# Row projection with running-maximum record count: 384-row tiles in four slots and one hardware loop per engine, in place of 512-row tiles in three slots

## The chip, the cores and the metric

The kernel runs on one core of one Trainium2 chip. The metric is the device time of one execution in microseconds; lower is better. Most times below are medians of 4 or 5 executions. A ratio is the mean time of one kernel's fast runs over that of the other's fast runs of the same rounds, so it is not quite the ratio of the medians. Engines: PE multiplies matrices, DVE, ACT and POOL work on vectors, SP issues nearly all transfers. A *slot* is a buffer in SBUF that holds one tile. *Queued* means issued and not yet landed.

## The reference

```python
B, S, D = 8, 2048, 4096              # float32
proj = (x @ w).squeeze(-1)           # x: B,S,D   w: D,1
cm = np.maximum.accumulate(proj, axis=1)
is_record = (proj >= cm).astype(np.float32)
return np.cumsum(is_record, axis=1)
```

Each of the 16,384 rows of x (16 KB each, 268.4 MB in all) is read once and multiplied with one vector. The result is 64 KB. There are two float32 operations for every 4 bytes read, so reading x is the first suspect for the limit.

## The kernel before

Positions 0 to 1919 of each batch are handled in four *groups* of 512, 512, 512 and 384 positions. A group has eight tiles, one per batch. Each of the 128 partitions takes r neighbouring rows of a tile, so one transfer has 128 pieces of r x 16 KB. The last 128 positions (the tail) come in tiles of 64 positions of 2 batches.

```python
RS = (4, 4, 4, 3)          # rows per partition in each group
NS = 3                     # slots of R = 4 rows: 3 x 64 KB per partition
VC = 2816                  # DVE takes columns 0..2815, POOL and ACT the rest

def at(g, t):              # the slot of tile t of group g
    return xbuf[(t if g < NL else t + NS - 1) % NS]

def user_before(g, t):     # the tile that must be finished before t may overwrite its slot
    if t >= NS:
        return t - NS, g + 1
    if g == NL:
        return B - NS + t, g
    return max(u for u in range(B) if u % NS == t), g

# SP, in this order; SP blocks at each wait
i = SY.dma_start(out=at(g, t)[:, : r * D], in_=x[...].rearrange("(p r) d -> p (r d)", r=r)
    ).then_inc(xs[t], 16)
u, n = user_before(g, t)
if n: i._wait_ge(*(free(u, n)))

# DVE: one product with a sum for each row; "go" starts POOL on the tile
for t in range(B):
    if r == R:
        V.wait_ge(xs[t], 16).then_inc(go, 1)      # 512-row groups: when the tile has landed
    for j in range(r):
        i = dot(...)
        if j == 0 and r < R:
            i._wait_ge(xs[t], 16).then_inc(go, 1) # last group: when DVE's first product ends
        elif j == 1:
            i.then_inc(xs[t], -16)
    i.then_inc(fr[t], 1)
# POOL multiplies the other columns, ACT sums them, and then the slot is free.
# ... (cut: PE brings a group's sums into rows; DVE does two scans and a compare; the tail)

with V.Fori(0, NL): ...    # a hardware loop for the three 512-row groups on each engine,
group_dots(RS[-1], NL)     # the last group written out behind it
```

A hardware loop uses the same addresses in each pass, so in the first three groups tile t always sits in slot t mod 3. Eight tiles are no multiple of three. At a group boundary, tile 0 therefore waits for tile 6 of the group before, not for tile 5, which is free one tile earlier.

## Time and profile before

The kernel before takes 631.57 us (median of 3 executions, 631.42 to 631.84). The first fence holds lines of its profile's page: the span, the busy tenths of the 16 DMA engines in 40 slices, the packets, the instruction packets, the costliest groups (busy us, mean ns | idle us before, and what ended it), and the transfers (count, KB each where it is one size under 8 MB, median us from issue to landing).

```profile
span 630.0 us, 1182 instructions
...
DMA  9999999999999999999999999999999999999995
...
DMA packets 6579, 268.55 MB, mean 426 GB/s; under 512 B 768, under 2 KB 1040, under 8 KB 1584
...
q14 instruction: 3, 0.02, 0.0%
...
L127 DVE CUSTOM_DVE_ANT_0 xall<-xall,w_v 128x2816 f32<-128x2816 f32 (+3 forms) x133 | 388.4, 2974 | 187.8 <-DMA xall<-in_x_dram 187.8
L287 POOL TENSOR_TENSOR xall<-xall,w_sb 128x1280 f32<-128x1280 f32 x120 | 344.9, 2909 | 250.2 <-POOLq L290 250.2
...
xall<-in_x_dram SPq DMA_DIRECT2D x8, 6144.0 KB, 30.5
...
xall<-in_x_dram SPq DMA_DIRECT2D x24, 45.0
```

Read the DMA row first: full from the first slice to the last but one. DVE's wait line agrees: it waits for data and nothing else in front of its products.

The timeline of DVE shows the rhythm (start us, duration us, engine, line, operation; in brackets the idle time before it and what ended it). First two neighbouring 512-row tiles, then two 384-row tiles of the last group:

```profile
198.15 3.09 DVE L127 CUSTOM_DVE_ANT_0 xall<-xall,w_v 128x2816 f32<-128x2816 f32 x1 [6.52 <-DMA xall<-in_x_dram]
...
217.50 3.09 DVE L127 CUSTOM_DVE_ANT_0 xall<-xall,w_v 128x2816 f32<-128x2816 f32 x1 [7.23 <-DMA xall<-in_x_dram]
...
512.69 3.09 DVE L127 CUSTOM_DVE_ANT_0 xall<-xall,w_v 128x2816 f32<-128x2816 f32 x1 [5.42 <-DMA xall<-in_x_dram]
...
527.24 3.09 DVE L127 CUSTOM_DVE_ANT_0 xall<-xall,w_v 128x2816 f32<-128x2816 f32 x1 [5.43 <-DMA xall<-in_x_dram]
```

8 MiB each 19.35 us and 6 MiB each 14.55 us (14.53 in most pairs) are both 433 GB/s. The Trainium skill, page "DMA: Bandwidth & Descriptors", section "Where 436 GB/s comes from", gives 435.2 GB/s as the ceiling of the 16 SBUF ports. The trace agrees to half a per cent, so I take the stream to be at its ceiling: only time in which it moves fewer bytes can be lost or won.

This is the first group boundary: ACT finishes tile 6, SP then issues tile 0 of the next group, and tile 7 is taken up by DVE.

```profile
151.58 1.27 ACT L133 ACTIVATE xall<-xall 128x1280 f32<-128x1280 f32 x1 [1.50 <-POOL xall L287]
...
152.97 0.33 SPq L171 DMA_DIRECT2D xall<-in_x_dram  x1
...
159.44 3.09 DVE L127 CUSTOM_DVE_ANT_0 xall<-xall,w_v 128x2816 f32<-128x2816 f32 x1 [7.23 <-DMA xall<-in_x_dram]
```

When tile 0 is issued at 152.97, only tile 7 is still in the queue, and it lands within 6.5 us (DVE takes it at 159.44). Inside a group about a tile more, some 26 us in all, is queued at each issue.

### The profile page before, as it was taken

The page shows a single profiled execution, that of the slowest core. Times are in us where ns is not written, and L with a number is a line of the kernel's source. Part 1 is how long each engine was busy: PE and PEld are TensorE (multiplying, and loading weights), DVE is VectorE, ACT ScalarE, POOL GpSimd, SP SyncE. Part 2 cuts the span into 40 slices and gives each one's busy share as a digit, 9 for nine tenths or more (in the row PEclk, how much of TensorE's full clock was granted, in tenths as well). Part 3 has the DMA queues.
Part 4 walks back from the last instruction along what each step waited for, and adds up shares of the span by engine and source line. Part 5 has one row for each costly group of instructions (what it writes and reads, how often), then busy time and mean ns, then how long its engine had stood idle before and what let it go on. Part 6 is the DMA issues. An engine that isn't in the chain of part 4 may idle for free.

```text
span 630.0 us, 1182 instructions
## 1 busy us (share of the span) xinstructions
PE 31.7 (5%) x108; PEld 15.1 (2%) x108; DVE 406.9 (65%) x292; ACT 180.4 (29%) x273; POOL 370.1 (59%) x147
## 2 busy tenths in 40 slices
PE   8000000000010000000010000000002000000031
PEld 3000000000010000000010000000001000000010
DVE  0755676546785557755579555676557966655897
ACT  1222332123322233222233222332223232232353
POOL 0555676446765557755567555576555766666685
PEclk9999999999999999999996555555555555555555
DMA  9999999999999999999999999999999999999995
GB/s 400 399 466 399 466 408 458 421 442 433 433 441 424 445 424 441 425 445 420 449 416 454 412 458 408 458 408 458 408 425 437 444 418 437 444 415 440 416 424 230
DMA packets 6579, 268.55 MB, mean 426 GB/s; under 512 B 768, under 2 KB 1040, under 8 KB 1584
## 3 DMA queue, kind: packets, MB, share of 16 engines
q1 hardware_dynamic: 6560, 268.50, 98.8%
q10 hardware_dynamic: 16, 0.02, 0.0%
q14 instruction: 3, 0.02, 0.0%
HBM read 268.45 MB, written 0.07 MB: 426 GB/s over the span
## 4 chain that ended last, share of the span: by engine, by line
POOL 52%; issue 38%; DMA 6%; PE 2%; DVE 1%; SPq 0%; POOLq 0%; ACT 0%; ACTq 0%
POOL xall L287 52%; DMA xall<-in_x_dram 6%; PE w_v L231 2%; PE ps L231 0%; DVE xall L127 0%; SPq L199 0%; DMA w<-in_w_dram 0%; POOLq L290 0%; ACT w L242 0%; PE ps L373 0%; DVE cm_l L143 0%; DVE cnt_l L149 0%; DVE ps L146 0%; ACT xall L133 0%; DVE masked L365 0%
## 5 line engine op out<-in xcount | busy, mean ns | idle before, releaser
L127 DVE CUSTOM_DVE_ANT_0 xall<-xall,w_v 128x2816 f32<-128x2816 f32 (+3 forms) x133 | 388.4, 2974 | 187.8 <-DMA xall<-in_x_dram 187.8
L287 POOL TENSOR_TENSOR xall<-xall,w_sb 128x1280 f32<-128x1280 f32 x120 | 344.9, 2909 | 250.2 <-POOLq L290 250.2
L133 ACT ACTIVATE xall<-xall 128x1280 f32<-128x1280 f32 (+1 forms) x130 | 162.8, 1252 | 429.7 <-POOL xall L287 417.1
L319 PE MATMUL ps<-identity,small 128*8 128x128 f32 x60 | 13.1, 410 | 572.0 <-PEq L316 572.0
L133 ACT ACTIVATION_READ_ACCUMULATOR xall<-xall 128x1 f32 x130 | 24.2, 186 | 0.0
L343 POOL TENSOR_TENSOR xall<-xall,w_sb 128x1280 f32<-128x1280 f32 (+1 forms) x8 | 21.6, 2704 | 2.8 <-DMA xall<-in_x_dram 2.8
L319 PEld LDWEIGHTS ps<-identity,small 128*8 128x8 f32 x60 | 7.5, 128 | 578.8 <-issue 574.8
L143 DVE TENSOR_TENSOR_SCAN cm<-ps,cm,small 8x512 f32<-8x512 f32 (+1 forms) x5 | 6.1, 1216 | 14.1 <-PE ps L319 14.1
L231 PE MATMUL w_v<-w,identity 8*128 8x512 f32 x14 | 12.1, 1056 | 0.0
L127 DVE DVE_READ_ACCUMULATOR2_ANT small<- 128x1 f32 x133 | 10.8, 82 | 0.0
L253 DVE MEMSET ps<- 8x512 f32 x1 | 0.5, 485 | 15.5 <-ACT w L242 15.5
L149 DVE TENSOR_TENSOR_SCAN cnt<-ps,cnt,small 8x512 f32<-8x512 f32 (+1 forms) x5 | 6.1, 1217 | 0.2
L373 PE MATMUL ps<-fold,masked 128*8 128x64 f32 x32 | 4.6, 303 | 20.1 <-ACT masked L361 13.2
L231 PEld LDWEIGHTS w_v<-w,identity 8*128 8x128 f32 x14 | 4.6, 332 | 7.3 <-issue 7.3
L239 ACT COPY w_sb<-w_v 128x768 f32<-128x768 f32 x1 | 0.8, 799 | 11.4 <-PE w_v L231 11.4
L146 DVE TENSOR_TENSOR ps<-ps,cm 8x512 f32<-8x512 f32 (+1 forms) x5 | 3.3, 660 | 0.2
L373 PEld LDWEIGHTS ps<-fold,masked 128*8 128x8 f32 x32 | 2.5, 112 | 22.4 <-ACT masked L361 14.6
L361 ACT ACTIVATE masked<-fold,small 128x8 f32<-128x8 f32 x9 | 2.5, 297 | 0.2
L231 PE MATMUL ps<-w,identity 8*128 8x512 f32 x2 | 2.1, 1136 | 2.6 <-DMA w<-in_w_dram 2.6
L238 ACT ACT_TABLE_LOAD x1 | 1.3, 1283 | 2.7 <-DVE fold L249 2.7
L245 DVE TENSOR_REDUCE fold<-identity 128x2 f32<-128x128 f32 x1 | 0.3, 286 | 2.1 <-POOL cnt L224 2.1
L343 POOL TENSOR_TENSOR xall<-xall,w 128x352 f32<-128x352 f32 (+1 forms) x2 | 1.5, 766 | 0.2 <-DMA xall<-in_x_dram 0.2
(23 smaller groups left out, 7.0 us busy)
## 6 DMA issues: line engine op xcount, KB each, us to landing
xall<-in_x_dram SPq DMA_DIRECT2D x8, 6144.0 KB, 30.5
xall<-in_x_dram SPq DMA_DIRECT2D x6, 2048.0 KB, 39.5
xall<-in_x_dram SPq DMA_DIRECT2D x1, 1200.0 KB, 33.5
xall<-in_x_dram SPq DMA_DIRECT2D x1, 848.0 KB, 35.1
xall<-in_x_dram SPq DMA_DIRECT2D x1, 752.0 KB, 36.3
xall<-in_x_dram SPq DMA_DIRECT2D x1, 576.0 KB, 37.1
xall<-in_x_dram SPq DMA_DIRECT2D x24, 45.0
xall<-in_x_dram SPq DMA_DIRECT2D x1, 352.0 KB, 17.4
```

What stands on the lines that cost most here:

```text
L127: return V.tensor_tensor_reduce(out=xsl, in0=xsl, in1=wsl, scale=1.0, scalar=0.0, op0=ALU.mult, op1=ALU.add, accum_out=dst,)
L133: return A.activation(out=xsl, in_=xsl, func=ACTF.Copy, accum_out=dst)
L143: V.tensor_tensor_scan(out=cm_, data0=src, data1=low, initial=cm0, op0=ALU.max, op1=ALU.max,)._wait_ge(psr, base).then_inc(psr, 1)
L146: V.tensor_tensor(out=src, in0=src, in1=cm_, op=ALU.is_ge)._wait_ge(psr, base + 1).then_inc(psr, 1)
L149: V.tensor_tensor_scan(out=cnt_, data0=src, data1=low, initial=cnt0, op0=ALU.add, op1=ALU.max,)._wait_ge(psr, base + 2).then_inc(cs, 1)
L231: i = T.matmul(out=dst, lhsT=identity[:NW, k : k + 1].to_broadcast([NW, P]), rhs=w_row, start=True, stop=True,).then_inc(bw, 1)
L238: A.copy(out=w_sb[:, CV - VC :], in_=ps)._wait_ge(bw, 1).then_inc(wc, 1)
L287: i = G.tensor_mul(out=xl, in0=xl, in1=w_sb).then_inc(pl, 1)
L319: i = T.matmul(out=ps[:B, j : r * P : r], lhsT=l[:, j * B : (j + 1) * B], rhs=identity, start=k == 0, stop=k == 1,)
L343: G.tensor_mul(out=xl, in0=xl, in1=w_pool(*p))._wait_ge(xq[i], 16).then_inc(pl, 1)
L361: A.activation(out=e, in_=on, func=ACTF.Copy, scale=acc)._wait_ge(*wait).then_inc(ms, 1)
L373: return T.matmul(out=ps[:B, q : q + Q], lhsT=e, rhs=by_i, start=start, stop=bool(stop),)._wait_ge(*((mg, on_g) if pool else (ms, on_a)))
```

## The change

All 1920 positions go in five equal groups of 384 positions with four slots (192 KiB per partition as before). Eight tiles are a multiple of four, so tile 0 of a group waits for tile 4 of the group before. One loop on each engine covers all groups, and the program gets shorter. Side effects: POOL starts every tile only when DVE's first product of it ends, and the tail's tiles wait for tiles 4 to 6 of the last group.

```diff
-    RS = (4, 4, 4, 3)
+    RS = (3, 3, 3, 3, 3)
-    NS = 3
+    NS = 4
     def at(g, t):
-        return xbuf[(t if g < NL else t + NS - 1) % NS]
+        return xbuf[t % NS]
     def user_before(g, t):
-        if t >= NS:
-            return t - NS, g + 1
-        if g == NL:
-            return B - NS + t, g
-        return max(u for u in range(B) if u % NS == t), g
+        return (t - NS, g + 1) if t >= NS else (t + B - NS, g)
 ...
         def slot(m):                      # where tail tile m goes, and whose slot that was
-            if m < NS:
-                return None, xbuf[m][:, RS[-1] * D :]
-            u = B - NS if m < 2 * NS else B - NS + 1
-            return u, at(NL, u)[:, (m % NS) * D : (m % NS + 1) * D]
+            u = B - NS + m // R
+            return u, at(NG, u)[:, m % R * D : (m % R + 1) * D]
 ...
-                if r == R:
-                    V.wait_ge(xs[t], 16).then_inc(go, 1)
                 for j in range(r):
                     i = dot(...)
-                    if j == 0 and r < R:
+                    if j == 0:
                         i._wait_ge(xs[t], 16).then_inc(go, 1)
 ...
-        with V.Fori(0, NL):
+        with V.Fori(0, NG):
             ...
-        group_scans()                     # the written-out last group goes,
-        V.sem_inc(psr, -3)                # on DVE, POOL, ACT and PE alike
-        group_dots(RS[-1], NL)
```

More of the change, by code (lines that the diff above doesn't have):

```diff
@@ L41 @@
     NW = D // WC
-    RS = (4, 4, 4, 3)
+    RS = (3, 3, 3, 3, 3)
     R = RS[0]
-    NS = 3
+    NS = 4
     NG = len(RS)
-    NL = NG - 1
     N = R * P
@@ L189, in slot @@
         def slot(m):
-            if m < NS:
-                return None, xbuf[m][:, RS[-1] * D :]
-            u = B - NS if m < 2 * NS else B - NS + 1
-            return u, at(NL, u)[:, (m % NS) * D : (m % NS + 1) * D]
-        freed = {None}
+            u = B - NS + m // R
+            return u, at(NG, u)[:, m % R * D : (m % R + 1) * D]
+        freed = set()
         for i, (m, c0, c1, _, _) in enumerate(TILES):
@@ L292 @@
         G.wait_ge(wc, 3)
-        with G.Fori(0, NL):
+        with G.Fori(0, NG):
             group_products(R)
-        group_products(RS[-1], NL)
         def group_sums(r, g=0):
@@ L307, in group_sums @@
             A.wait_ge(pd, 1).then_inc(pd, -1)
-        with A.Fori(0, NL):
+        with A.Fori(0, NG):
             group_sums(R)
-        group_sums(RS[-1], NL)
         def group_rows(r):
@@ L324, in group_rows @@
                         i.then_inc((pd, psr)[k], 1)
-        with T.Fori(0, NL):
+        with T.Fori(0, NG):
             group_rows(R)
-        group_rows(RS[-1])
         nv = npool = na = nm = on_a = on_g = 0
```

## The prediction

> **What bounds the kernel now.** The input stream. The page shows the DMA engines at 9 tenths or more in every slice but the last, 268.45 MB read from HBM, 426 GB/s over the span of 630.0 us. The table of stretches shows a DMA share of 0.99 to 1.02 from 4 to 623 us. In the timeline of DVE, 512-row tiles (8 MiB) become ready every 19.35 us and the 384-row tiles of the last group (6 MiB) every 14.53 us; both are 433 GB/s. The Trainium skill, page "DMA: Bandwidth & Descriptors", section "Where 436 GB/s comes from", states 435.2 GB/s as the ceiling of the 16 SBUF ports; the trace agrees to half a per cent. DVE is busy 65%, POOL 59%, ACT 29%. The chain of waits names POOL for 52%, but POOL only waits for tiles: it idles 7.8 us between two, and DVE waits for DMA 32 times, 187.8 us in all.
>
> **What the change does.** Bytes, products, the 192 KiB of buffers per partition and the tail's tiles stay. Tile transfers go from 24 of 8 MiB plus 8 of 6 MiB to 40 of 6 MiB.
> - Cost per transfer: 19.35 and 14.53 us fit t = bytes/435 GB/s + about 0.07 us. Hence 40 x 14.53 = 581.2 us instead of 24 x 19.35 + 8 x 14.53 = 580.6: +0.56 us (estimate from these intervals). This alone is on the critical path.
> - POOL now starts a tile when DVE's first product ends, as in the last group of before. A tile is done about 2.97 + 3 x 2.87 + 1.45 = 13.0 us after landing, under the 14.53 us period. DVE needs 9.2 us.
> - Group boundaries: between the last product and the next, DVE loses about 8 us today (PE rows, two scans, a compare); it delays one tile, and DVE catches up within two.
> - Slack: when a slot comes free, about 7 + 19 = 26 us of transfers are queued ahead now, and 1.5 + 14.5 + 14.5 = 30 us then. The queue runs dry in neither, so the fourth slot and the smaller grain buy nothing.
> - Tail: its tiles now wait for the last group's tiles 4, 5 and 6. At each of these moments some 30 us is still queued, so the stream doesn't break. The 7 us after the last landing are the same code.
> - Instruction fetches: the trace has three 8 KB packets on the instruction queue in mid-run. Around the first two, tiles landed 0.2 and 0.7 us late, the only clearly irregular intervals. The program gets shorter (no unrolled last group), so up to 0.9 us could come back, but I can't tell which engine fetches, on which DMA engine.
>
> **Prediction.** 631.57 + 0.56 - about 0.6 = 631.5 us. Range 630.7 to 632.5 us. Faster by over 2%: 0.01. Within 2%: 0.98. Slower by over 2%: 0.01.
>
> **What would show it.** Tile-ready intervals of 14.53 us in all five groups; 40 issues of 6144 KB, some 45 us from issue to landing; DMA share near 1.0 up to about 623 us; DVE's waits for DMA about 40, totalling some 190 us; slots freed with over 25 us still queued; last landing at 622 to 624 us; 7 us after it. POOL's idle time before a tile about 5.9 us.
>
> **What would make it wrong.** A hole in the DMA share at a group boundary or at the start of the tail (SyncE waiting for a slot with the queue empty), tile intervals above 14.6 us in the earlier groups (HBM addresses at other offsets), or POOL or ACT falling behind at five boundaries. Each would be slower. Faster by much isn't possible while every byte is read once through the same ports.

## The result and the profile after

The changed kernel takes 632.37 us (632.36 to 632.46, 4 runs) against 631.58 us (631.42 to 631.84, 4 runs): ratio 1.0012, interval [0.9995, 1.003]. The result is the same within 2%. The interval includes 1, but no run of the changed kernel was under any of the kernel before in that comparison; the repeats below (5 runs, 632.34 to 632.45, against 9 runs of before, 631.29 to 632.16) show the same order. So there is a difference of about +0.8 us, or 0.12%, in medians.

The same lines of the page of the changed kernel:

```profile
span 630.3 us, 1211 instructions
...
DMA  9999999999999999999999999999999999999996
...
DMA packets 7747, 268.55 MB, mean 426 GB/s; under 512 B 904, under 2 KB 1208, under 8 KB 1728
...
q14 instruction: 3, 0.02, 0.0%
...
L126 DVE CUSTOM_DVE_ANT_0 xall<-xall,w_v 128x2816 f32<-128x2816 f32 (+3 forms) x133 | 389.0, 2973 | 171.8 <-DMA xall<-in_x_dram 171.8
L275 POOL TENSOR_TENSOR xall<-xall,w_sb 128x1280 f32<-128x1280 f32 x120 | 344.4, 2897 | 251.0 <-POOLq L278 251.0
...
xall<-in_x_dram SPq DMA_DIRECT2D x40, 6144.0 KB, 45.0
```

The DMA row is as full as before. The bytes are the same, in 7747 packets instead of 6579; 1024 of the added 1168 are data: 40 x 128 = 5120 pieces of 48 KB in place of 24 x 128 of 64 KB and 8 x 128 of 48 KB. The timelines of DVE and POOL in the second group:

```profile
193.13 3.09 DVE L126 CUSTOM_DVE_ANT_0 xall<-xall,w_v 128x2816 f32<-128x2816 f32 x1 [5.43 <-DMA xall<-in_x_dram]
...
207.73 3.09 DVE L126 CUSTOM_DVE_ANT_0 xall<-xall,w_v 128x2816 f32<-128x2816 f32 x1 [5.48 <-DMA xall<-in_x_dram]
```

```profile
196.31 8.60 POOL L275 TENSOR_TENSOR xall<-xall,w_sb 128x1280 f32<-128x1280 f32 x3 [5.92 <-POOLq L278]
```

Tiles come every 14.53 us in all groups (14.60 in this pair: most likely the 12 KB store of results, issued with tile 4 of each group). POOL starts 3.2 us after DVE and idles 5.9 us before a tile. At the first group boundary SP issues tile 0 at 89.83, 30 us before tile 7 is taken up at 120.25:

```profile
89.83 0.33 SPq L166 DMA_DIRECT2D xall<-in_x_dram  x1
...
120.25 3.09 DVE L126 CUSTOM_DVE_ANT_0 xall<-xall,w_v 128x2816 f32<-128x2816 f32 x1 [5.42 <-DMA xall<-in_x_dram]
```

The critical chain ends in the same way in both kernels: DVE's last wait for data ends at 623.36 (623.09 before), 7 us before the end. The last transfers of the tail land while DVE is still at work, the very last at 625.2 (624.9 before).

### The profile page after: what moved, and what is told of

Read it like the earlier page. It is cut to its first block, busy times and chain, and to the rows that moved or that the text cites. A ratio compares the mean times of both kernels' runs of the same rounds, so it can differ in the third digit from the quotient of the medians.

```text
span 630.3 us, 1211 instructions
## 1 busy us (share of the span) xinstructions
PE 32.2 (5%) x108; PEld 15.0 (2%) x108; DVE 407.1 (65%) x295; ACT 180.3 (29%) x273; POOL 369.6 (59%) x147
## 2 busy tenths in 40 slices
DMA packets 7747, 268.55 MB, mean 426 GB/s; under 512 B 904, under 2 KB 1208, under 8 KB 1728
## 4 chain that ended last, share of the span: by engine, by line
POOL 51%; issue 38%; DMA 6%; PE 2%; DVE 1%; SPq 0%; POOLq 0%; ACT 0%; ACTq 0%
POOL xall L275 51%; DMA xall<-in_x_dram 6%; PE w_v L224 2%; DMA w<-in_w_dram 0%; DVE xall L126 0%; PE ps L224 0%; SPq L192 0%; POOLq L278 0%; ACT w L235 0%; PE ps L358 0%; DVE cm_l L142 0%; DVE cnt_l L148 0%; DVE ps L145 0%; ACT xall L132 0%; POOLq L281 0%
## 5 line engine op out<-in xcount | busy, mean ns | idle before, releaser
L126 DVE CUSTOM_DVE_ANT_0 xall<-xall,w_v 128x2816 f32<-128x2816 f32 (+3 forms) x133 | 389.0, 2973 | 171.8 <-DMA xall<-in_x_dram 171.8
L142 DVE TENSOR_TENSOR_SCAN cm<-ps,cm,small 8x384 f32<-8x384 f32 x6 | 6.0, 1004 | 29.1 <-PE ps L305 29.1
L148 DVE TENSOR_TENSOR_SCAN cnt<-ps,cnt,small 8x384 f32<-8x384 f32 x6 | 6.0, 1004 | 0.2
L145 DVE TENSOR_TENSOR ps<-ps,cm 8x384 f32<-8x384 f32 x6 | 3.3, 554 | 0.2
L358 PEld LDWEIGHTS ps<-fold,masked 128*8 128x8 f32 x32 | 2.5, 112 | 22.3 <-ACT masked L346 14.6
```

The costliest lines, as they stand in the source:

```text
L126: return V.tensor_tensor_reduce(out=xsl, in0=xsl, in1=wsl, scale=1.0, scalar=0.0, op0=ALU.mult, op1=ALU.add, accum_out=dst,)
L142: V.tensor_tensor_scan(out=cm_, data0=src, data1=low, initial=cm0, op0=ALU.max, op1=ALU.max,)._wait_ge(psr, base).then_inc(psr, 1)
L145: V.tensor_tensor(out=src, in0=src, in1=cm_, op=ALU.is_ge)._wait_ge(psr, base + 1).then_inc(psr, 1)
L148: V.tensor_tensor_scan(out=cnt_, data0=src, data1=low, initial=cnt0, op0=ALU.add, op1=ALU.max,)._wait_ge(psr, base + 2).then_inc(cs, 1)
L358: return T.matmul(out=ps[:B, q : q + Q], lhsT=e, rhs=by_i, start=start, stop=bool(stop),)._wait_ge(*((mg, on_g) if pool else (ms, on_a)))
```

## The experiments

The first four ran on one chip, the next four in another, and the last four in a third. Each has its own runs of the kernel before: medians 631.70, 631.75 and 631.79, so the chips hardly differ.

### Error bars: both kernels again

No edit.

> The kernel before, unchanged, for a second trace and an error bar. Theory (the excess is instruction fetches on the queue): ratio 1.000 within 0.0007; again two tile intervals of the first group are long by 0.2 to 0.7 us, and instruction packets of 8 KB stand at the same moments. Rival (these were chance): the irregular intervals are elsewhere or gone, and the time moves by up to 0.9 us.

> The changed kernel, unchanged. Theory (stream-bound, 40 transfers each with a fixed cost of 0.07 us, fetches as in its first trace): 0.3 to 0.9 us slower than before, ratio 1.0005 to 1.0014, tile intervals of 14.53 us. Rival (no difference at all, only noise): ratio 1.000, interval on both sides of it.

Measured: before_again 631.59 us (631.47 to 631.67, ratio 0.9998, interval [0.9985, 1.0012]); after_again 632.37 us (632.34 to 632.45, ratio 1.0011, interval [0.9998, 1.0025]). The +0.8 us repeats in medians, though the intervals alone don't settle it. In the second trace of the kernel before, the two long intervals of the first group are there again (19.66 and 19.63 us), beside instruction packets at 116.3 and 126.0 us; in its first trace they were 19.59 and 20.05 us. Two traces have them at the same place, so they are part of this kernel and not chance. The longest, in the first trace:

```profile
120.04 3.09 DVE L127 CUSTOM_DVE_ANT_0 xall<-xall,w_v 128x2816 f32<-128x2816 f32 x1 [7.46 <-DMA xall<-in_x_dram]
...
140.09 3.09 DVE L127 CUSTOM_DVE_ANT_0 xall<-xall,w_v 128x2816 f32<-128x2816 f32 x1 [7.93 <-DMA xall<-in_x_dram]
```

### What an added packet costs, and what an added transfer costs

packets3: each partition takes three rows that lie 128 apart, so a transfer has three packets of 16 KB per partition instead of one of 48 KB. The result stays correct. (The addresses read change too. In the second run they stay the same, but there packets and transfers grow together.)

```diff
-    out=at(g, t)[:, : r * D],
-    in_=x[...].rearrange("(p r) d -> p (r d)", r=r)
+    out=at(g, t)[:, : r * D].rearrange("p (r d) -> p r d", r=r),
+    in_=x[...].rearrange("(r p) d -> p r d", r=r)
 ...
-    out=ps[:B, j : r * P : r]
+    out=ps[:B, j * P : (j + 1) * P]
```

> The changed kernel with each partition taking three rows that lie 128 rows apart, so each transfer has three packets of 16 KB per partition instead of one of 48 KB; transfers, bytes and work are the same, and the result stays right. Theory A (the fixed 0.07 us of a transfer is per packet, 0.009 us each on a DMA engine): 16 more packets per tile and engine, 14.67 us per tile, 5.6 us longer than the changed kernel (about 638). Theory B (it is per transfer, its closing semaphore write): no change, 632.4.

transfers2: each tile is fetched by two transfers of half of each partition's columns.

```diff
-    i = SY.dma_start(out=at(g, t)[:, : r * D], in_=src).then_inc(xs[t], 16)
+    i = SY.dma_start(out=at(g, t)[:, :H1], in_=src[:, :H1]).then_inc(xs[t], 16)   # waits for the slot
+    SY.dma_start(out=at(g, t)[:, H1 : r * D], in_=src[:, H1:]).then_inc(xs[t], 16)
 ...
-    i._wait_ge(xs[t], 16).then_inc(go, 1)
+    i._wait_ge(xs[t], 32).then_inc(go, 1)         # and -32 in place of -16
```

> The changed kernel with each tile fetched by two transfers of 3 MiB (half of each partition's columns), 80 in place of 40. Both theories of the 0.07 us: once more 8 packets and one transfer per tile, so 14.60 us per tile, 2.8 us longer than the changed kernel (about 635.2). Rival (the difference of the two kernels has nothing to do with the number of transfers): no change, 632.4.

Measured: packets3 638.20 us (ratio 1.0103), transfers2 635.54 us (ratio 1.0060), against after_again 632.37 us. The page's packet line of packets3, and two tiles in its timeline of DVE:

```profile
DMA packets 17987, 268.55 MB, mean 422 GB/s; under 512 B 904, under 2 KB 1208, under 8 KB 1728
```

```profile
194.53 3.09 DVE L126 CUSTOM_DVE_ANT_0 xall<-xall,w_v 128x2816 f32<-128x2816 f32 x1 [5.57 <-DMA xall<-in_x_dram]
...
209.27 3.09 DVE L126 CUSTOM_DVE_ANT_0 xall<-xall,w_v 128x2816 f32<-128x2816 f32 x1 [5.63 <-DMA xall<-in_x_dram]
```

10,240 more packets, 640 on each of the 16 DMA engines, cost 5.83 us, or 0.0091 us each. (The two lines are 14.74 us apart with a store between them; most pairs are 14.68 or 14.69 apart; 14.67 was forecast.) In transfers2, 320 more packets per engine at that price make 2.9 of the 3.2 us, so 40 more transfers cost next to nothing by themselves. Both accounts forecast transfers2 alike; what tells them apart is packets3, which would have cost nothing had the cost been of the transfer. So the fixed cost in the prediction is of the packet; that the changed addresses in packets3 cost the same by chance is not excluded by a run. The intervals alone give 0.0097 us (14.69 against 14.53) and 0.0094 us (14.61): the total of packets3 is a little smaller because its stream begins some 0.8 us earlier. The change adds 64 data packets per engine (1024 / 16): 0.58 us, where the prediction said 0.56. The Trainium skill, page "DMA: Bandwidth & Descriptors", section "Measured (HBM→SBUF, 128 partitions, SWDGE, issued from GpSimd)", puts about 10.5 ns on a packet from a software-generated transfer of 4 KB with 64 packets. It doesn't say how many engines these were spread over, so the two figures are not the same measure: 9 to 10 ns here are for each packet on its engine, with hardware-generated packets of 16 to 48 KB.

### Do instruction fetches cost the stream?

unrolled: the loops are written out five times on each engine.

```diff
-        with V.Fori(0, NG):      # and so for G, A and T
+        for _ in range(NG):
```

> The changed kernel with the hardware loops replaced by five written-out copies of their bodies on every engine: same work, a longer program. Theory (fetches of 8 KB cost the stream 0.2 to 0.7 us each because they use a DMA engine): some 4 to 7 more packets on the instruction queue, each beside a tile interval longer than 14.53 us, in total 1 to 4 us longer than the changed kernel. Rival (fetches cost the stream nothing): 632.4 and even intervals.

Measured: 633.69 us (ratio 1.0029, interval [1.0016, 1.0043]), 1.3 us over the changed kernel (632.37 on another chip; the same kernel with POOL started early, below, took 632.47 on a third). The instruction line of the page, and the long interval in the timeline of DVE:

```profile
q14 instruction: 7, 0.06, 0.0%
```

```profile
382.12 3.09 DVE L126 CUSTOM_DVE_ANT_0 xall<-xall,w_v 128x2816 f32<-128x2816 f32 x1 [1.05 <-DMA xall<-in_x_dram]
...
397.62 3.09 DVE L126 CUSTOM_DVE_ANT_0 xall<-xall,w_v 128x2816 f32<-128x2816 f32 x1 [6.38 <-DMA xall<-in_x_dram]
```

15.50 us instead of 14.53, with two 8 KB instruction packets at 387 and 389 us. By the landings, the fetches at 123 and 143 us go with 0.14 and 0.11 us, one late in the tail with 0.3 us; those at 186 and 594 us leave no mark beyond 0.01 us. Together 1.5 us, against 0.2 to 0.3 us in the two traces of the changed kernel: the difference is the 1.3 us. (slots3_rotating, below, is written out too and has the same seven packets and again one interval of 15.50 us.) The count and the total were as the theory had them; that each packet has a long interval beside it was not. With the 0.7 us beside the fetch at 126.4 us in the first trace of the kernel before, a fetch costs the stream between nothing and 0.7 us.

The packed traces show why (the landings of each semaphore, which no view above prints). Every transfer raises its semaphore 16 times, presumably once for each of the 16 DMA engines, and a tile is ready at the last rise. Where one fetch falls between two tiles, one of the 16 rises comes 0.65 to 1.0 us late and stays late in the tiles after it; the other 15 keep their places. The tile is delayed only by what this rise comes after the rise that was last. At 186 us a rise 0.03 us after the first moves to 0.71, and the last stays at 1.28: nothing is lost. At 387 and 389 us two rises move to 1.83 and 2.20, past the last at 1.26: 0.97 us are lost. The packet itself takes 0.3 us; why the rise moves by more is open.

The Trainium skill, page "Runtime: NRT & Kernel Launch", section "Instruction fetch mechanics", calls the cost of crossing from one block of instructions to the next mostly hidden. No run here measures that cost on the fetching engine; what shows here is a cost to a stream that uses the same DMA engines and has no time to spare.

### Do the slots matter?

slots3 is the changed kernel with three slots, with the rule of the kernel before for whom tile 0 waits for.

```diff
-    NS = 4
+    NS = 3
     def user_before(g, t):
-        return (t - NS, g + 1) if t >= NS else (t + B - NS, g)
+        if t >= NS: return t - NS, g + 1
+        return max(u for u in range(B) if u % NS == t), g
```

> The changed kernel with three slots of 384 rows in place of four. Theory (when a slot comes free, 1.5 + 14.5 = 16 us of transfers are still queued, enough): within 0.5 us of the changed kernel, tiles every 14.53 us, 31 us from issue to landing. Rival (the fourth slot carries part of the result, and paid back a loss from the smaller tiles): several us slower.

Measured: 646.94 us, ratio 1.0238. My theory missed, and the rival came true: several us slower, here 14.6. The DMA row of its page, and its timeline around the first group boundary (all engines, cut):

```profile
DMA  9999999999999989999999899999989999999995
```

```profile
117.69 1.27 ACT L132 ACTIVATE xall<-xall 128x1280 f32<-128x1280 f32 x1 [1.48 <-POOL xall L277]
...
119.08 15.42 SPq L168 DMA_DIRECT2D xall<-in_x_dram  x3
120.40 3.09 DVE L126 CUSTOM_DVE_ANT_0 xall<-xall,w_v 128x2816 f32<-128x2816 f32 x1 [5.41 <-DMA xall<-in_x_dram]
```

Inside a group nothing is wrong: tiles come every 14.53 us. Tile 0 of the next group, however, waits for tile 6 and is issued at 119.08 (the line merges three issues), and tile 7, the only one still queued, is in DVE's hands at 120.40. So 1.3 us were queued, not 16. By the landings in the trace, tile 0 arrives 16.19 us after tile 7 and tile 1 another 16.22 us later (it waits for tile 7), 3.35 us lost in two steps, and 3.5 to 3.6 us at the three later boundaries. The table of stretches shows the hole (columns: stretch, its length, busy us of PE, PEld, DVE, ACT and POOL with counts, PE clock, DMA share, GB/s), first slots3, then the changed kernel:

```profile
118.00:124.00 6.00, 0.00 (x0) 0.00 (x0) 3.60 (x3) 1.06 (x2) 0.43 (x1) 1.00 0.77 272
```

```profile
118.00:124.00 6.00, 0.00 (x0) 0.00 (x0) 3.75 (x3) 0.89 (x2) 0.57 (x1) 1.00 0.92 395
```

Three runs test this reading. slots3_rotating uses the three slots strictly in turn over all 40 tiles, with written-out loops, so that tile 0 waits for tile 5:

```diff
-        return xbuf[t % NS]
+        return xbuf[(g * B + t) % NS]            # NS = 3
-        with V.Fori(0, NG): group_dots(R)
+        for g in range(NG): group_dots(R, g)     # likewise the other engines
```

> Three slots of 384 rows, but used strictly in turn over all 40 tiles (8 tiles are no multiple of 3, so the loop bodies are written out, as in the run unrolled), so that each tile waits for the tile three before it at group boundaries too. Theory (slots3 lost 3.4 us at each of four boundaries because the first tile of a group waited for tile 6 instead of tile 5, with 1.5 us of transfers left in the queue): the four losses go, and the time is that of unrolled, 633.7, within 1 us. Rival (three slots of this size are too few whatever the order): about 647 to 648 again.

Measured: 633.48 us (633.48 to 633.69, ratio 1.0028), the time of unrolled with four slots (633.69), and not 647. At the same boundary tile 0 is now issued with 15.9 us queued:

```profile
104.58 0.33 SPq L166 DMA_DIRECT2D xall<-in_x_dram  x1
...
120.45 3.09 DVE L126 CUSTOM_DVE_ANT_0 xall<-xall,w_v 128x2816 f32<-128x2816 f32 x1 [5.42 <-DMA xall<-in_x_dram]
```

Three slots are enough; the order in which they are reused was the fault.

slots3_early_pool keeps the bad order and starts POOL when a tile lands, so that tile 6 is free sooner:

```diff
+                V.wait_ge(xs[t], 16).then_inc(go, 1)
                 for j in range(r):
-                    if j == 0:
-                        i._wait_ge(xs[t], 16).then_inc(go, 1)
-                    elif j == 1:
+                    if j == 1:
```

> Three slots of 384 rows in the order of slots3, with POOL started when a tile lands. Theory (what counts is how much is queued when the first tile of a group is issued, against some 3 to 5 us that an issue to an empty queue costs): tile 6 is free 10.1 us after landing, 4.4 us are left in the queue in place of 1.5, so the boundary losses shrink from 3.4 to about 0 to 1 us each: 632.4 to 636. Rival (the loss is of the boundary's computing, not of the queue): 644 or more.

Measured: 632.71 us (ratio 1.0013). The timeline at the same boundary:

```profile
115.93 0.33 SPq L168 DMA_DIRECT2D xall<-in_x_dram  x1
...
120.59 3.09 DVE L126 CUSTOM_DVE_ANT_0 xall<-xall,w_v 128x2816 f32<-128x2816 f32 x1 [5.55 <-DMA xall<-in_x_dram]
```

With 4.5 us queued in place of 1.3, the later boundaries lose nothing; the first loses 0.4 us, with instruction fetches close by.

early_pool is the same edit with the change's four slots:

> The changed kernel (four slots), with POOL started when a tile lands. Theory (with four slots some 30 us are queued at every issue, so 3 us of POOL are no matter): 632.4 within 0.3 us, the same as the changed kernel. Rival (the late start of POOL is what makes the changed kernel slower by 0.1%): 631.6.

Measured: 632.47 us (632.38 to 632.63), ratio 1.0011, as the changed kernel. With four slots POOL's late start costs nothing, and it isn't the source of the +0.8 us.

### Two slots

slots2 and slots2_early_pool leave two slots for the groups; the tail has room of its own, so these two differ from the others in the tail as well.

```diff
-    NS = 4
+    NS = 2                   # slots 2 and 3 are kept for tail tiles 0 to 5
+    # slots2_early_pool: with the edit of slots3_early_pool as well
```

> The changed kernel with two slots of 384 rows for the groups (the tail keeps room of its own). Theory: when a slot comes free only 1.5 us of transfers are queued, less than the 2.7 us that the first issue took beyond its bytes, so two tiles take 13.1 + 17.2 us instead of 29.1: 15.15 us per tile, and some 5 to 8 us more at each group boundary: 25 to 70 us longer than the changed kernel, DMA share visibly below 1. Rival (the queue's depth is no matter as long as the next transfer is issued): within 3 us.

> As slots2, but POOL starts a tile when it lands, not when DVE's first product ends (the wait on the landing is an instruction of its own again, as in the first three groups of before). Theory: a tile is done 10.1 us after landing instead of 13.0, so two tiles need 10.2 + 17.2 = 27.4 us, under 29.1: tiles every 14.53 us within a group, and only the four boundaries cost, 10 to 25 us in all; clearly faster than slots2. Rival (POOL's start is no matter here either): the same as slots2.

Measured: slots2 691.58 us (ratio 1.0951), slots2_early_pool 636.39 us (634.96 to 638.51, ratio 1.0066). Starting POOL 3 us earlier is worth 55 us here and nothing with four slots. The first is within its range. In its trace the queue ran dry once in each group: a tile issued 0.4 to 1.5 us after the one before had landed took 3.0 to 3.4 us longer than 14.53 us to land. The second missed its range (10 to 25 us) on the good side, with 4.0 us over the changed kernel. Its trace is of the slowest of the four executions. There the boundaries from the second on cost nothing (29.06 us for the pair); the losses are 3.3 us in the first group, 1.1 us at the first boundary and 1.5 us in single tiles later. Tile 2 was issued with 2.8 us queued and lost 2.0 us. With 4.3 to 4.4 us queued, tiles up to the first boundary lost up to 1.1 us, and nearly all later ones nothing. Why the same depth costs differently is open.

### How close the kernel before was to this

before_late_pool is the kernel before with POOL started as in the change.

```diff
-                if r == R:
-                    V.wait_ge(xs[t], 16).then_inc(go, 1)
-                    if j == 0 and r < R:
+                    if j == 0:
```

> The kernel before (three slots of 512 rows), with POOL started only when DVE's first product of the tile ends, as the change has it. Theory: tile 6 is free 16.1 us after landing instead of 13.1, so at the two boundaries inside the loop only 3.3 us instead of 6.2 are queued when the next group's first tile is issued: 0 to 3 us lost at each, 631.6 to 638, tile intervals even elsewhere. Rival (the kernel before has slack of a whole tile at each issue, as the prediction said): 631.6.

Measured: 634.97 us (633.94 to 635.44), ratio 1.0048, interval [1.0034, 1.0062]. The timeline at its first boundary, to be set beside the one of the kernel before:

```profile
156.49 0.33 SPq L171 DMA_DIRECT2D xall<-in_x_dram  x1
...
159.77 3.09 DVE L127 CUSTOM_DVE_ANT_0 xall<-xall,w_v 128x2816 f32<-128x2816 f32 x1 [7.23 <-DMA xall<-in_x_dram]
```

3.3 us were queued in place of 6.5, and tiles 0 and 1 land 1.2 and 0.1 us late at this boundary and 1.0 and 0.5 us late at the next, 2.8 of the 3.2 us (634.97 against 631.79). The intervals elsewhere were not as even as the theory had it: in the first group three are 0.2 to 0.7 us long (two in the kernel before). The kernel before had a margin of one POOL delay at its group boundaries, not of a whole tile.

## Why the prediction was right or wrong, point by point

The time, 632.37 us, lies inside the range of 630.7 to 632.5, near its upper end; the class (within 2%) was right. The point forecast of 631.5 us was a hair under the kernel before, and the change came out 0.8 us over it, so the sign of the small difference was wrong. The class follows from the stream; that the sum came within 0.9 us owes something to luck, as the points on fetches and start below show.

- **Stream-bound at the ceiling: right.** Even intervals of 14.53 us, a full DMA row, 7 us from DVE's last wait for data to the end (the very last landing, at 625.2, is a little later than the 622 to 624 us forecast); early_pool shows that POOL's timing is off the critical path.
- **+0.56 us for smaller transfers: right in size, the cause sharpened.** packets3 and transfers2 put 0.0091 us on each packet, which makes 0.58 us for the change. I had called it a cost per transfer.
- **-0.6 us from fewer irregular fetches: its size was right, its reason and its effect on the total not.** Both kernels have three instruction packets in the span, so none went away. From the second tile to the last group's last tile, the second traces show 0.86 us over the plain sum of intervals before (22 x 19.353 + 8 x 14.533 = 542.03, measured 542.89), and none after (38 x 14.533 = 552.25, measured 552.24); some 0.2 us of the 0.86 are result stores. The first trace of the changed kernel still had one interval 0.2 us long, and in its second trace a fetch in the tail cost 0.26 us. This gain was eaten by the next item.
- **Missed: a later start.** Subtracting two plain intervals from DVE's second tile, the stream begins at 3.6 to 3.7 us in the kernels with 64 KB packets and at 3.9 to 4.6 us in those with 48 KB packets, although the first packet starts at 2.0 us in all. In the second traces this is +0.56 us (+0.29 in the first). The landings narrow it: less one plain interval, the first of the 16 rises of the first tile's semaphore comes at 2.9 to 3.0 us in both kernels, but the last follows it by 0.4 to 0.7 us before and by 0.9 to 1.1 us after. So the 16 parts of the stream are further apart from the start on. That also leaves more room for a fetch to hide, as with the fetch at 122.5 us in the second trace (a rise moves by 0.68 us, the last stays), so the lost start and the gain from the fetches are not independent. Small packets alone are not the reason: packets3, with 16 KB, has the closest parts (0.4 us) and begins at 3.3 us. A further 0.25 us of the +0.78 us lies outside the span of the trace (632.34 against a span of 630.3; 631.59 against 629.8). With 0.58 us for the packets, these terms (+0.58 - 0.86 + 0.26 + 0.56 + 0.25) add up to the 0.8 us of the second traces. What sets the spread at the start and the time outside the span is open; no run isolated it.
- **"When a slot comes free, about 26 us are queued ahead now ... The queue runs dry in neither": the number was wrong, the conclusion for these two kernels right.** Inside a group it holds. At the boundaries inside the loop of the kernel before only 6.5 us were queued, which is enough (before_late_pool, with 3.3 us, loses 3.2 us in all).
- **"So the fourth slot and the smaller grain buy nothing": wrong as reasoning.** The smaller tiles with POOL's late start, in three slots and a loop, cost 14.6 us (slots3), and the fourth slot gives exactly that back, because four divides eight and tile 0 then waits for tile 4. Written-out loops with rotating slots (slots3_rotating) or an early POOL (slots3_early_pool) remove the same loss without a fourth slot. The change was neutral because two parts of opposite effect came together.
- **Tail waits and group boundaries of the changed kernel: right**, with 30 us queued at each boundary. DVE's waits for DMA were 39, in all 171.8 us, a little less than forecast, as the first tile of a group is there before DVE is ready.

No kernel tried beats the kernel before. With its bytes at that rate, what is left inside the stream is about a microsecond of fetches and packets.

## What to carry to other kernels

When a transfer stream is at its ceiling, changing tile size or slot count moves only crumbs: count packets (0.009 us each here) and instruction fetches, and expect little (here a tenth of a per cent). Judge the depth of a queue where the order of slots breaks, not in the steady state: if the tiles per pass of a hardware loop are no multiple of the slots, the first tile of the next pass waits for a later slot than it needs, and one tile of depth is gone. Before calling a part of a change useless, take it away: here the fourth slot repaid a 14.6 us loss that the smaller tiles brought with them.

## What the Trainium skill lacked or had wrong

- Page "DMA: Bandwidth & Descriptors", section "Measured (HBM→SBUF, 128 partitions, SWDGE, issued from GpSimd)": a cost per packet in nanoseconds is given only for one small software-generated transfer (about 10.5 ns; elsewhere the page counts a few cycles for each packet). Hardware-generated packets of 16 to 48 KB cost 9 to 10 ns each on their DMA engine at full stream rate (640 more for each engine: +5.83 us), and a transfer costs next to nothing by itself while others are queued.
- The same page gives a fixed cost of about 2 us for one software-generated transfer, and no rule for how much must be queued to hide such a cost. Here an issue with 1.3 us queued cost the stream 1.7 to 2.0 us (slots3), one with 3.3 us queued 1.0 to 1.2 us (before_late_pool), and with 4.3 to 4.5 us it was mostly nothing, but up to 1.1 us (slots2_early_pool).
- Page "Runtime: NRT & Kernel Launch", section "Instruction fetch mechanics": the cost of crossing to the next block is told as mostly hidden, and a cost to a stream on the DMA engines is not mentioned. With the DMA engines at their ceiling, an 8 KB fetch delayed one of the 16 parts of the stream by 0.65 to 1.0 us and the stream by 0 to 0.7 us, and writing out the loops cost 1.3 us in all. The page speaks of 16 KiB blocks; the traces show packets of 8 KB, some of them alone (whether two make a block was not shown).
- No page that I read has the slot-order rule: tiles per loop pass not divisible by the slots cost one tile of queue depth at each pass (+14.6 us here).
